# Hybrid encoder layer on one core: decay tables by column halves, q and k turned before they are split, side work on GpSimd

## The chip, the cores and the metric

The kernel runs on 1 core of one Trainium2 chip. The metric is the device time in microseconds (us) from launch to the end of the program; lower is better. Each kernel is timed in several runs, of which the median counts, and one further execution is profiled.

## The reference: what is computed

One encoder layer over 1024 tokens of width 1024 in float32. Only the middle part matters here:

```
u = x @ W_in  -> [q | k | v | z | x_ssd | B | C | dt_fwd | dt_bwd]
a = GQA(qk-RMSnorm, 2-D axial rotary, bidirectional)       # 8 query heads of 64, 2 key heads
s = bidirectional Mamba-2 SSD(conv, chunked scan per direction, summed, + D skip, SiLU(z) gated RMSNorm)
x = LN1(alpha*x + concat(a, s) @ W_out)
...
seg = a_cum[..., :, None] - a_cum[..., None, :]             # in each chunk of 128 tokens, each of 8 heads
Lmat = jnp.exp(jnp.where(tril, seg, -jnp.inf))              # the decays
y_diag = jnp.einsum('bcgls,bgrcls,bcsgrp->bclgrp', cb, Lmat, xd)
```

Ahead of it stands a SwiGLU block with a LayerNorm, behind it a second one, a gated embedding and the last LayerNorm. They take most of the time, and the change leaves them alone.

## The kernel before, in words

Matmuls of float32 accuracy are made of three single-pass products: each operand is split into a high part (a rounding copy, on ScalarE, written ACT in the profile) and a low part (the difference, `lo`, line 87, on VectorE, written DVE). `mm3` (line 122) issues high times low, low times high and high times high. TensorE (PE) follows the order in which the program is written: an `in_order` wrapper around the whole of `run` chains its instructions. The order on the other engines and on the DMA queue (SP) is set by a scheduler that plans with a simulated timeline; `behind` pins an instruction behind the last one traced on an engine. PSUM holds two pools: `big` with two buffers of two banks (`psb`) and `sm` with four buffers of one bank (`pss`).

**q and k** (`qkv_part`). Eight products of 128 tokens for q (512 columns, 24 matmuls each), then eight for k, v and dt (272 columns, 24 matmuls each). For each tile of tokens `step` runs the turn of an earlier tile, `front` (square, sum, power on GpSimd), the low part of an earlier tile and `back` (`rope`: Newton steps on the root, scaling by it at line 852, rotary). The result was split while tokens lay on the partitions: q into `qs` (high and low side by side), k into `kd`, where each head stands twice. Then `turn` transposed high and low together: eight transposes for a tile of q (line 901, into `big`), four for a tile of k (line 884, into `sm`), and one ScalarE copy brought them into Q (line 902) or K (line 885). A head of Q has its high part on partitions 0 to 63 and its low part on 64 to 127; K holds the high part on both halves for j = 0 and the low part for j = 1, so that two matmuls sum all four products.

**The convolved branch** (`xbc_part`) has eight products of 48 matmuls. The last turns of k ran between the halves of the first.

**Attention.** 64 steps of 128 queries of one head. A step has four score matmuls (line 1151), a maximum over 1024 keys on DVE (line 1158), the exponential on ACT (line 1160), the turn of an earlier step (eight transposes, line 1173, two ACT copies, two low parts on DVE) and a quarter of the product with V (lines 1188 and 1189). After four steps a head is done: ACT copies one half of the PSUM result to `a_tmp` (line 1195) and DVE adds the other (line 1196). After two heads GpSimd (POOL) spreads the reciprocal sums to `rx` (line 1201), and `normalise` turns them by a float32 matmul with the identity (line 1210); DVE multiplies (line 1211), POOL splits the result (lines 1213 and 1214). The list `aside` is worked off one entry in every second step, behind ACT and DVE: the SiLU of the last z tile (`one_more`, four reciprocals, `silu`), the SSD tables (`turned`, `masks`) and the splits of eight blocks of W_out.

**SSD, right to left** (`ssd_right`). For each of eight chunks and each direction a pair of banks got, for four heads at a time, a bf16 matmul of the identity with the mask (line 1342) and one of `LT` with `RT` (line 1343): 59 rows of the contraction carry the cumulative sums. ACT takes the exponential of 1024 columns (line 1345). Behind that come C times B (line 1349), the part from the state (lines 1262 and 1264), the next state (line 1273; its scaling on ACT at line 1256) and the product with x (line 1366). Products with half of W_out (`spilled`) lie between, two at the start and one at the end.

Of the kernel before, what the change touches and what calls it, by code (L numbers as in the profile page):

```python
# [9 lines left out]
F32 = mybir.dt.float32  # L10
F32R = mybir.dt.float32r
# [16 lines left out]
NQ = 8  # L28
# [8 lines left out]
class Layer:  # L37
# [778 lines left out]
    def qkv_part(self, c, xT):  # L816
# [30 lines left out]

        def rope(v, nh, m, ss, r, nm, t):

            self.newton(r, ss, nh)  # L850
            qn = wk.tile([P, nh, HD], F32, name="qn")
            nc.vector.tensor_tensor(out=qn, in0=v, in1=r.unsqueeze(2).broadcast_to([P, nh, HD]), op=ALU.mult)  # L852
# [8 lines left out]
            return qn  # L861

        NK = NKV * HD
        late = []

        def kv_front(t, ps):
# [5 lines left out]
            return st  # L872

        def kv_back(t, st):

            kn = rope(*st, "k", t).unsqueeze(2).broadcast_to([P, NKV, 2, HD])
            kd = wk.tile([P, NKV, 2, 2, HD], F32R, name="qs", bufs=4)
            nc.scalar.copy(out=kd[:, :, 0], in_=kn)

            def turn():  # L880
                pt = self.pss().rearrange("p (g j t) -> p g j t", g=NKV, j=2)
                for g in range(NKV):
                    for j in range(2):
                        nc.tensor.transpose(out=pt[:, g, j], in_=kd[:, g, j].rearrange("p a d -> p (a d)").bitcast(F32), identity=self.ident)  # L884
                nc.scalar.copy(out=K[:, :, :, t * P:(t + 1) * P], in_=pt)
            late.append(turn)
            return kd[:, :, 1], kn, kd[:, :, 0]

# [3 lines left out]
        def q_back(t, st):  # L892
            qs = wk.tile([P, NQ, 2, HD], F32R, name="qs", bufs=4)
            qn = rope(*st, "q", t)
            nc.scalar.copy(out=qs[:, :, 0], in_=qn)

            def turn():
                pt = self.psb().rearrange("p (h t) -> p h t", t=P)
                qv = qs.bitcast(F32)
                for hh in range(NQ):  # L900
                    nc.tensor.transpose(out=pt[:, hh], in_=qv[:, hh].rearrange("p a d -> p (a d)"), identity=self.ident)
                nc.scalar.copy(out=Q[:, :, t * P:(t + 1) * P], in_=pt)
            late.append(turn)
            return qs[:, :, 1], qn, qs[:, :, 0]

        backs, los = [], []

        def step(t, ps, front, back, keep=1):


            if len(late) > keep or not front:
                late.pop(0)()
            st = front(t, ps) if front else None
            if los:
                self.lo(*los.pop())
            if backs:
                los.append(backs.pop()())
            if front:
                backs.append(lambda: back(t, st))

# [11 lines left out]
        self.pend += [lambda: step(NT, None, None, None)] * 4  # L932
        self.x0 = self.xbc_gemm(0, xT, 1)
# [94 lines left out]
    def z_last(self, xT, aside):  # L1028

        nc, V = self.nc, self.nc.vector  # L1030
        ps = self.z_product(NT - 1, xT)
        r = self.ring.tile([P, 1024], F32, name="blk")
        z, e = r[:, :512], r[:, 512:]
        V.tensor_copy(z, ps)
        nc.scalar.activation(out=e, in_=ps, func=AF.Exp, scale=-1.0)

        def one_more():
            V.tensor_scalar(out=e, in0=e, scalar1=1.0, scalar2=None, op0=ALU.add)

        def invert(m):  # L1040
            V.reciprocal(e[:, m], e[:, m])

        def silu():
            V.tensor_tensor(out=z, in0=z, in1=e, op=ALU.mult)
            nc.sync.dma_start(out=self.zd[NT - 1], in_=z)
        aside += [one_more, *(lambda m=slice(i * P, (i + 1) * P): invert(m) for i in range(4)), silu]
# [78 lines left out]
    def attention(self, c, mixT, aside, begin):  # L1125
# [53 lines left out]
        def values(u, part):  # L1179
# [13 lines left out]
            raw, rsum = st[qh, hp]["raw"], st[qh, hp]["rsum"]  # L1193
            tmp = ev.tile([64, 512], F32, name="a_tmp")
# [9 lines left out]
        def normalise():  # L1204
            if "norm" not in st:
                return
            qh, hp, rx, raw = st.pop("norm")
            R = self.pss()
            for qt in range(4):
                nc.tensor.matmul(R[:, qt * P:(qt + 1) * P], lhsT=rx[:, qt].rearrange("p h d -> p (h d)"), rhs=self.ident, start=True, stop=True)  # L1210
            nc.vector.tensor_tensor(out=raw, in0=raw, in1=R, op=ALU.mult)
            hi, lo = (x[:, hp] for x in mixT[qh][0])
            nc.gpsimd.tensor_copy(hi, raw)
            nc.gpsimd.tensor_tensor(out=lo, in0=raw, in1=hi.bitcast(F32), op=ALU.subtract)
# [71 lines left out]
    def ssd_tables(self, pool):  # L1286


        nc, I, V = self.nc, self.I, self.nc.vector

        G = nc.gpsimd
        self.LT = LT = [pool.tile([P, NT, P], BF16, name=f"LT{d}") for d in range(2)]
        self.RT = [pool.tile([P, 8, P], BF16, name=f"RT{b}") for b in range(2)]
        self.mask = pool.tile([P, 2, P], BF16, name="mask")
        self.idb = pool.tile([P, P], BF16, name="idb")
        rraw, mraw = (self.ring.tile([P, 8, P], F32, name="blk") for n in range(2))
        nc.sync.dma_start(out=rraw[:59], in_=I["rows"])
        nc.sync.dma_start(out=mraw[:, :2], in_=I["mask"])
        for d in range(2):
            G.memset(LT[d], 0.0)  # L1300
            G.memset(LT[d][32 * d:32 * d + 3], 1.0)
            for i in range(3):
                nc.sync.dma_start(out=LT[d][32 * d + 3 + 8 * i:32 * d + 11 + 8 * i], in_=self.sc[1][d, i].rearrange("c h l -> h c l"))
        for b in range(2):
            G.memset(self.RT[b], 0.0)
        dsk = pool.tile([P, 16], F32, name="dsk")
        nc.sync.dma_start(out=dsk[:, :8], in_=I["d_skip"].broadcast_to([P, 8]))
        self.dsk = dsk[:, :8]

        def turned(ch):  # L1310
            V.tensor_copy(self.RT[ch % 2][:59], rraw[:59])
            self.rows(ch)

        def masks():
            V.tensor_copy(self.mask, mraw[:, :2])
            V.tensor_copy(self.idb, self.ident)
        return [lambda: turned(NT - 1), lambda: turned(NT - 2), masks]

    def ssd_right(self, c, loaded, fillers):
# [5 lines left out]
        self.accr = c.enter_context(tc.tile_pool(name="accr", bufs=2))  # L1325
        LT, RT, mask, idb, dsk = self.LT, self.RT, self.mask, self.idb, self.dsk
        for ch in (NT - 1, NT - 2):
            loaded[ch] = self.chunk(ch)

        def front(ch):  # L1330
# [7 lines left out]
            for d in range(2):  # L1338
                pD = self.psb()
                for n in range(2):  # L1340
                    o = pD[:, n * 512:(n + 1) * 512]
                    nc.tensor.matmul(o, lhsT=idb, rhs=mask[:, d].unsqueeze(1).broadcast_to([P, 4, P]), start=True, stop=False)
                    nc.tensor.matmul(o, lhsT=LT[d][:, ch], rhs=rt[:, n * 4:n * 4 + 4], start=False, stop=True)
                e = ep.tile([P, 8, P], F32, name=("Ef", "Eb")[d], bufs=2 + d)
                nc.scalar.activation(out=e.rearrange("p a b -> p (a b)"), in_=pD, func=AF.Exp)
                E.append(e)
# [179 lines left out]
    def run(self):  # L1526
# [37 lines left out]
        with ExitStack() as c:  # L1564
# [309 lines left out]
def host_arrays(inputs):  # L1874
# [54 lines left out]
    A["mask"] = c(np.stack([(1 - le) * np.float32(NEG), (1 - le.T) * np.float32(NEG)], 1))  # L1929
    rows = np.zeros((59, 8, P), np.float32)  # L1930
    for part in range(3):
# [27 lines left out]
```

## Time and profile before

| | |
|---|---|
| median of 3 runs | 1966.9 us (1966.21 to 1967.77) |
| span of the profiled execution, first to last instruction | 1962.3 us |
| q products, 715 to 766 us | PE busy 50.26 of 51 |
| k, v and dt products, 766 to 790 us | PE busy 23.47 of 24 |
| attention, one stretch of it, 900 to 940 us | PE 40.00 and DVE 39.94 of 40 |
| SSD right to left, 1070 to 1120 us | PE 50.00, ACT 42.86, DVE 40.01 of 50 |

The profiled execution has no time of its own beside its span; the median stands 4.6 us above the span, and this is what lies around it. A row of the timeline gives start, duration, engine, line, operation, output and inputs, the count where neighbours are merged, and in brackets the idle time ahead with what ended it. PE matmuls overlap in the records: a matmul shown with 0.39 us may be followed by the next after 0.23 us, so its price is the distance between starts. "SPq" is an issue on the DMA queue.

### The profile page before, as it was taken

The page shows a single profiled execution, that of the slowest core. Times are in us where ns is not written, and L with a number is a line of the kernel's source. Part 1 is how long each engine was busy: PE and PEld are TensorE (multiplying, and loading weights), DVE is VectorE, ACT ScalarE, POOL GpSimd, SP SyncE. Part 2 cuts the span into 40 slices and gives each one's busy share as a digit, 9 for nine tenths or more (in the row PEclk, how much of TensorE's full clock was granted, in tenths as well). Part 3 has the DMA queues.
Part 4 walks back from the last instruction along what each step waited for, and adds up shares of the span by engine and source line. Part 5 has one row for each costly group of instructions (what it writes and reads, how often), then busy time and mean ns, then how long its engine had stood idle before and what let it go on. Part 6 is the DMA issues. An engine that isn't in the chain of part 4 may idle for free.

```text
span 1962.3 us, 25749 instructions
## 1 busy us (share of the span) xinstructions
PE 1938.6 (99%) x9196; PEld 1614.3 (82%) x9196; DVE 1533.1 (78%) x2378; ACT 879.7 (45%) x1509; POOL 392.8 (20%) x292
## 2 busy tenths in 40 slices
PE   8999999999999999999999999999999999999998
PEld 7888888888888889888888888788888888888886
DVE  7977776867668658759998878997777777787698
ACT  7433333334444224538887775643333334443311
POOL 0144544430001132000101001003545440001011
PEclk9999999999999999999999999999999999999999
DMA  8434544559865112231003383253545439986122
GB/s 303 136 124 154 192 177 145 193 187 377 282 226 172 65 42 68 87 111 45 7 1 98 116 292 114 86 179 138 185 146 202 159 135 336 341 267 220 39 75 97
DMA packets 147180, 309.95 MB, mean 158 GB/s; under 512 B 17665, under 2 KB 30337, under 8 KB 147052
## 3 DMA queue, kind: packets, MB, share of 16 engines
q1 hardware_dynamic: 147052, 308.31, 44.9%
q8 instruction: 72, 1.18, 0.3%
q14 instruction: 56, 0.46, 0.1%
HBM read 216.83 MB, written 91.42 MB: 157 GB/s over the span
## 4 chain that ended last, share of the span: by engine, by line
PE 90%; DVE 6%; DMA 1%; POOL 1%; issue 1%; ACT 1%; SPq 0%; DVEq 0%; ACTq 0%; POOLq 0%
PE sm L122 56%; PE big L508 12%; PE sm L508 9%; PE big L122 3%; PE big L1151 2%; PE sm L1173 2%; DVE nm L1158 1%; PE sm L1188 1%; PE sm L1189 1%; POOL qr L845 1%; PE sm L1366 1%; PE sm L1262 1%; PE sm L1273 1%; DVE ptl L87 1%; DVE xl L87 1%
## 5 line engine op out<-in xcount | busy, mean ns | idle before, releaser
L122 PE MATMUL sm<-xh,blk 128*128 128x512 f32 x1424 | 439.9, 389 | 0.0
L122 PEld LDWEIGHTS sm<-xh,blk 128*128 128x128 f32 x1424 | 267.3, 188 | 55.4
L122 PE MATMUL sm<-xl,blk 128*128 128x512 f32 x736 | 283.9, 389 | 3.8 <-DVE xl L87 3.8
L122 PE MATMUL sm<-blk,xl 128*128 128x512 f32 (+2 forms) x784 | 238.4, 371 | 0.9 <-DVE qn L852 0.5
L122 PE MATMUL sm<-blk,xh 128*128 128x512 f32 (+2 forms) x584 | 202.7, 379 | 0.0
L108 ACT CAST blk<-raw 128x512 fp32r<-128x512 f32 (+1 forms) x168 | 101.1, 610 | 213.2 <-PE sm L122 128.6
L87 DVE TENSOR_TENSOR blk<-s,blk 128x512 fp32r<-128x512 f32 x176 | 152.1, 869 | 35.4 <-ACT blk L108 34.3
L87 DVE TENSOR_TENSOR blk<-raw,blk 128x512 fp32r<-128x512 f32 (+1 forms) x168 | 145.8, 871 | 37.9 <-ACT blk L108 37.5
L108 ACT CAST blk<-s 128x512 fp32r<-128x512 f32 x172 | 105.7, 622 | 138.9 <-PE sm L122 122.3
L122 PEld LDWEIGHTS sm<-xl,blk 128*128 128x128 f32 x736 | 138.2, 188 | 32.7 <-issue 4.2
L122 PEld LDWEIGHTS sm<-blk,xl 128*128 128x128 f32 x784 | 142.9, 188 | 25.3 <-PE sm L884 0.8
L178 POOL TENSOR_TENSOR ln_k<-ln_k,mhalf 128x1 f32<-128x1 f32 x32 | 36.9, 1158 | 583.2 <-DVE ln_k L177 578.2
L508 PE MATMUL big<-xh 128*128 128x512 f32 x576 | 138.8, 390 | 0.0
L267 POOL TENSOR_TENSOR s<-raw 128x512 f32<-128x512 f32 x34 | 55.1, 1621 | 387.4 <-DVE blk L87 294.3
L87 DVE TENSOR_TENSOR xh<-blk,xh 128x1024 fp32r<-128x1024 f32 x78 | 95.4, 1223 | 47.0 <-ACT xh L454 39.2
L454 ACT CAST xl<-blk 128x1024 fp32r<-128x1024 f32 x76 | 80.1, 1054 | 114.0 <-PE sm L508 43.2
L454 ACT CAST xh<-blk 128x1024 fp32r<-128x1024 f32 x78 | 82.2, 1054 | 106.7 <-PE big L508 47.4
L508 PEld LDWEIGHTS big<-xh 128*128 128x128 f32 x576 | 107.8, 188 | 22.2
L87 DVE TENSOR_TENSOR xl<-blk,xl 128x1024 fp32r<-128x1024 f32 x76 | 92.6, 1219 | 42.6 <-ACT xl L454 36.5
L122 PEld LDWEIGHTS sm<-blk,xh 128*128 128x128 f32 x584 | 109.8, 188 | 19.2
L508 PE MATMUL big<-xl 128*128 128x512 f32 x480 | 115.8, 390 | 0.0
L122 PE MATMUL sm<-xET3h,blk 128*128 128x512 f32 x352 | 108.4, 389 | 0.0
(339 smaller groups left out, 4025.3 us busy)
## 6 DMA issues: line engine op xcount, KB each, us to landing
raw<-in_wi_dram SPq DMA_DIRECT2D x81, 512.0 KB
blk<-hS SPq DMA_DIRECT2D x154, 256.0 KB
hS<-h SPq DMA_DIRECT2D x88, 256.0 KB
wr<-in_wo_dram SPq DMA_DIRECT2D x44, 512.0 KB
blk<-wT SPq DMA_DIRECT2D x88, 256.0 KB
hS<-sg SPq DMA_DIRECT2D x66, 256.0 KB
wT<-wr SPq DMA_DIRECT2D x66, 256.0 KB
blk<-in_wo_dram SPq DMA_DIRECT2D x66, 256.0 KB
```

The lines of the kernel that those rows point to most:

```text
L87: (eng or self.nc.vector).tensor_tensor(out=out, in0=full, in1=hi.bitcast(F32), op=ALU.subtract)
L108: self.nc.scalar.copy(out=b[:, 0, :n], in_=src)
L122: self.nc.tensor.matmul(ps, lhsT=a, rhs=b, start=(i == 0), stop=(i == n - 1))
L178: nc.gpsimd.tensor_tensor(out=r, in0=v, in1=self.mhalf[:, :1], op=ALU.pow)
L267: lambda: G.tensor_tensor(out=s1, in0=a21, in1=a22, op=ALU.add),
L454: A.copy(out=b[:, :, 0], in_=r)
L508: nc.tensor.matmul(ps[q], lhsT=b[:, 0, x, cut], rhs=b[:, 1, y], start=j == i == 0, stop=j == NP - 1 and i == 2)
L845: nc.gpsimd.tensor_tensor(out=r, in0=ss, in1=self.mhalf[:, :nh], op=ALU.pow)
L1151: nc.tensor.matmul(ps[:, n * 512:(n + 1) * 512], lhsT=Q[:, h, q0:q0 + P], rhs=K[:, h // 4, j, n * 512:(n + 1) * 512], start=j == 0, stop=j ...
L1158: nc.vector.tensor_reduce(out=nm, in_=ps, axis=AX.X, op=ALU.max, negate=True)
L1173: nc.tensor.transpose(out=pt[:, k], in_=pr[:, kk * P:(kk + 1) * P], identity=self.ident)
L1188: nc.tensor.matmul(po, lhsT=vw, rhs=pth[k // 4][:, k % 4], start=k == 0, stop=False)
```

## The change

- **q and k.** `rope` writes into a tile that is handed in and is split no more there. `turned` transposes four blocks of 128 columns of float32 into one `sm` buffer: a tile of q (four pairs of heads), or four tiles of k at once. ACT copies the high part from PSUM, and one step on, DVE takes the low part from PSUM; DMAs then put the pieces where Q and K want them: four for a tile of q (64 partitions, pieces of 512 bytes), eight for four tiles of k. Odd heads of Q now have the low part on top.
- **Attention.** ACT copies the other half of the result straight into `a_raw` in place of `a_tmp`. The sums are turned by a transpose in place of a matmul. `one_more`, `silu`, the copies for `RT`, the masks and the low parts of the eight blocks of W_out go to GpSimd.
- **Decays.** One matmul with all 128 rows serves all eight heads and half of the columns: rows 64 to 127 of `LT` hold the mask of that half and those of `RT` an identity, so the mask matmuls go. The exponential reads the banks as (half, head, column) and writes (head, half, column). `LT` has four tiles in place of two, with twelve DMAs in place of six.

```diff
+        def turned(blocks, place):
+            pt = self.pss()
+            for i, b in enumerate(blocks):
+                nc.tensor.transpose(out=pt[:, i * P:(i + 1) * P], in_=b, identity=self.ident)
+            hi, lo = (wk.tile([P, 512], F32R, name=n) for n in ("qhi", "qlo"))
+            nc.scalar.copy(out=hi, in_=pt)
+            def rest():
+                self.lo(lo, pt, hi)
+                for j, part in enumerate((hi, lo)):
+                    for e in range(2):
+                        for out in place(e, j):
+                            nc.sync.dma_start(out=out.bitcast(F32), in_=part[e * HD:(e + 1) * HD].bitcast(F32))
+            los.append(rest)
...
-            if len(late) > keep or not front:
+            if len(late) > keep:
                 late.pop(0)()
-            st = front(t, ps) if front else None
+            st = front(t, ps)
             if los:
-                self.lo(*los.pop())
+                los.pop()()
...
-            step(t, ps, kv_front, kv_back, 2)
+            step(t, ps, kv_front, kv_back, 1 if t < 2 else 0)
...
-            V.tensor_scalar(out=e, in0=e, scalar1=1.0, scalar2=None, op0=ALU.add)
+            nc.gpsimd.tensor_scalar(out=e, in0=e, scalar1=1.0, scalar2=None, op0=ALU.add)
...
-            nc.scalar.copy(out=tmp, in_=po[64:128])
-            nc.vector.tensor_tensor(out=raw[hh * 64:(hh + 1) * 64], in0=po[0:64], in1=tmp, op=ALU.add)
+            nc.scalar.copy(out=raw[mine], in_=po[other])
+            nc.vector.tensor_tensor(out=raw[mine], in0=po[mine], in1=raw[mine], op=ALU.add)
...
-                nc.tensor.matmul(R[:, qt * P:(qt + 1) * P], lhsT=rx[:, qt].rearrange("p h d -> p (h d)"), rhs=self.ident, start=True, stop=True)
+                nc.tensor.transpose(out=R[:, qt * P:(qt + 1) * P], in_=rx[:, qt].rearrange("p h d -> p (h d)"), identity=self.ident)
...
-                    nc.tensor.matmul(o, lhsT=idb, rhs=mask[:, d].unsqueeze(1).broadcast_to([P, 4, P]), start=True, stop=False)
-                    nc.tensor.matmul(o, lhsT=LT[d][:, ch], rhs=rt[:, n * 4:n * 4 + 4], start=False, stop=True)
+                    nc.tensor.matmul(pD[:, n * 512:(n + 1) * 512], lhsT=LT[d][n][:, ch], rhs=rt[:, :, n * 64:(n + 1) * 64], start=True, stop=True)
...
-                nc.scalar.activation(out=e.rearrange("p a b -> p (a b)"), in_=pD, func=AF.Exp)
+                nc.scalar.activation(out=e.rearrange("p h (n l) -> p n h l", n=2), in_=pD.rearrange("p (n h l) -> p n h l", n=2, h=8), func=AF.Exp)
...
-                aside.extend(lambda i=i, r=r: blocks0.append(self.split(r[:, i * 512:(i + 1) * 512])) for i in range(2) for r in early)
+                aside.extend(lambda i=i, r=r: blocks0.append(self.split(r[:, i * 512:(i + 1) * 512], eng=nc.gpsimd)) for i in range(2) for r in early)
```

More of the change, by code (lines that the diff above doesn't have):

```diff
@@ L872, in kv_front @@
             return st
+        kn = {}
         def kv_back(t, st):
[L876 to L887, printed above, removed]
+            h = t // 4
+            if t % 4 == 0:
+                kn[h] = wk.tile([P, 4, NKV, HD], F32, name="kn")
+            rope(kn[h][:, t % 4], *st, "k", t)
+            if t % 4 == 3:
+                cols = slice(h * 512, (h + 1) * 512)
+                late.append(lambda: turned([kn[h][:, i].rearrange("p g d -> p (g d)") for i in range(4)],
+                                           lambda g, j: [K[r * HD:(r + 1) * HD, g, j, cols] for r in range(2)]))
         def q_front(t, ps):
@@ L892, in q_back, with place @@
         def q_back(t, st):
[L893 to L906, printed above, removed]
+            qn = wk.tile([P, NQ, HD], F32, name="qn", bufs=4)
+            rope(qn, *st, "q", t)
+            Qv = Q.rearrange("p (i e) s -> p i e s", e=2)[:, :, :, t * P:(t + 1) * P]
+            def place(e, j):
+                r = e ^ j
+                return [Qv[r * HD:(r + 1) * HD, :, e]]
+            late.append(lambda: turned([qn[:, 2 * i:2 * i + 2].rearrange("p h d -> p (h d)") for i in range(4)], place))
         def step(t, ps, front, back, keep=1):
-            if len(late) > keep or not front:
+            if len(late) > keep:
                 late.pop(0)()
-            st = front(t, ps) if front else None
+            st = front(t, ps)
             if los:
-                self.lo(*los.pop())
+                los.pop()()
             if backs:
-                los.append(backs.pop()())
-            if front:
-                backs.append(lambda: back(t, st))
+                backs.pop()()
+            backs.append(lambda: back(t, st))
         tables("q", HD ** -0.5)
@@ L1286, in ssd_tables @@
     def ssd_tables(self, pool):
-        nc, I, V = self.nc, self.I, self.nc.vector
+        nc, I = self.nc, self.I
         G = nc.gpsimd
-        self.LT = LT = [pool.tile([P, NT, P], BF16, name=f"LT{d}") for d in range(2)]
+        self.LT = LT = [[pool.tile([P, NT, P], BF16, name=f"LT{d}{n}") for n in range(2)] for d in range(2)]
         self.RT = [pool.tile([P, 8, P], BF16, name=f"RT{b}") for b in range(2)]
-        self.mask = pool.tile([P, 2, P], BF16, name="mask")
-        self.idb = pool.tile([P, P], BF16, name="idb")
         rraw, mraw = (self.ring.tile([P, 8, P], F32, name="blk") for n in range(2))
-        nc.sync.dma_start(out=rraw[:59], in_=I["rows"])
-        nc.sync.dma_start(out=mraw[:, :2], in_=I["mask"])
+        nc.sync.dma_start(out=rraw, in_=I["rows"])
+        for n in range(2):
+            nc.sync.dma_start(out=mraw[64:, 2 * n:2 * n + 2], in_=I["mask"][64 * n:64 * n + 64])
         for d in range(2):
[L1300 to L1305, printed above, removed]
+            for n in range(2):
+                lt = LT[d][n]
+                G.memset(lt[:64], 0.0)
+                G.memset(lt[32 * d:32 * d + 3], 1.0)
+                for i in range(3):
+                    nc.sync.dma_start(out=lt[32 * d + 3 + 8 * i:32 * d + 11 + 8 * i], in_=self.sc[1][d, i].rearrange("c h l -> h c l"))
         dsk = pool.tile([P, 16], F32, name="dsk")
@@ L1310, in turned, with masks @@
         def turned(ch):
-            V.tensor_copy(self.RT[ch % 2][:59], rraw[:59])
+            G.tensor_copy(self.RT[ch % 2], rraw)
             self.rows(ch)
[L1314 to L1317, printed above, removed]
+        def masks(d):
+            for n in range(2):
+                G.tensor_copy(LT[d][n][64:], mraw[64:, 2 * n + 1 - d].unsqueeze(1).broadcast_to([64, NT, P]))
+        return [lambda: turned(NT - 1), lambda: turned(NT - 2), lambda: masks(0), lambda: masks(1)]
     def ssd_right(self, c, loaded, fillers):
@@ L1929, in host_arrays @@
     A["mask"] = c(np.stack([(1 - le) * np.float32(NEG), (1 - le.T) * np.float32(NEG)], 1))
-    rows = np.zeros((59, 8, P), np.float32)
+    rows = np.zeros((P, 8, P), np.float32)
+    for half in range(2):
+        rows[64 + np.arange(64), :, half * 64 + np.arange(64)] = 1.0
     for part in range(3):
```

15 lines of the change are left out of this document (6 added, 9 removed).

## The prediction, made before the result was known

> **What bounds the kernel now.** I read the page first, then the windows by stage, then the timeline of each stage that the diff touches.
>
> ```profile
> span 1962.3 us, 25749 instructions
> PE 1938.6 (99%) x9196; PEld 1614.3 (82%) x9196; DVE 1533.1 (78%) x2378; ACT 879.7 (45%) x1509; POOL 392.8 (20%) x292
> PE 90%; DVE 6%; DMA 1%; POOL 1%; issue 1%; ACT 1%; SPq 0%; DVEq 0%; ACTq 0%; POOLq 0%
> ```
> ```profile
> 900.00:940.00 40.00, 40.00 (x238) 33.73 (x236) 39.94 (x56) 32.95 (x62) 3.10 (x4) 1.00 0.02 8
> 1020.00:1070.00 50.00, 50.00 (x298) 42.73 (x297) 43.99 (x60) 39.05 (x71) 5.47 (x7) 1.00 0.18 53
> ```
>
> PE is busy 99% of the span and holds 90% of the chain that ended last, so a matmul taken out shortens the kernel unless another engine is nearly full in that stage. In a windows row the columns are length, then PE, PEld, DVE, ACT, POOL. DVE is full at 900 to 940 us and has slack at 1020 to 1070. PE's busy time overstates it, so I price every PE step by the distance between starts. The granted clock stays at 1.00 in these rows.
>
> **Turning q and k.**
>
> ```profile
> 732.97 1.03 PE L901 MATMUL big<-ident,qs 128*128 128x128 f32 x8
> 733.76 0.48 PE L122 MATMUL sm<-blk,xl 128*128 128x512 f32 x1
> ...
> 739.31 1.04 PE L901 MATMUL big<-ident,qs 128*128 128x128 f32 x8
> ...
> 769.62 0.60 PE L884 MATMUL sm<-ident,qs 128*128 128x128 f32 x4
> 769.97 0.37 PE L122 MATMUL sm<-blk,xl 128*128 128x272 f32 x1
> ```
>
> Eight transposes take 733.76 - 732.97 = 0.79 us, four 0.35. Each of the eight q tiles falls from eight to four: 8 x (0.79 - 0.35) = 3.5 us. For k, eight groups of four become two: 6 x 0.35 = 2.1 us, and the switch from transposes to another matmul costs PE something too, by estimate 0.05 a group. I take 2.4, bounds 2.1 and 2.6. The q step, 739.31 - 732.97 = 6.34 us, becomes 5.9.
>
> Two stalls of PE stand at the seam of q and k:
>
> ```profile
> 761.47 1.06 PE L901 MATMUL big<-ident,qs 128*128 128x128 f32 x8 [0.61 <-DVE qs L87]
> 766.53 0.36 PE L122 MATMUL sm<-blk,xl 128*128 128x272 f32 x1 [0.55 <-DVE qn L852]
> ```
>
> The first waits for a low part that the transposes no longer need; the second waits for a buffer of `sm`, and that pool now also holds what is turned of q. Steps get shorter, and the first turn of k comes one step behind its rope. I count the seam at nothing: at best both stalls go (1.2 us), at worst the first goes and the second comes four times as long (a loss of 1.1). The added DMAs, 8 x 4 and 2 x 8, go to SP behind low parts. Attention reads Q and K only behind the eight products of the convolved branch, so that transfer is covered; what the issues hold up is a rival below. ACT loses a copy of 1024 columns per q tile; GpSimd's power for the root is unchanged.
>
> **Attention.**
>
> ```profile
> 1030.74 1.08 PE L1151 MATMUL big<-K,Q 128*128 128x512 f32 x4
> ...
> 1033.47 1.08 PE L1151 MATMUL big<-K,Q 128*128 128x512 f32 x4
> ```
> ```profile
> 925.34 0.67 DVE L1211 TENSOR_TENSOR a_raw<-a_raw,sm 128x512 f32<-128x512 f32 x1
> ...
> 972.37 0.67 DVE L1211 TENSOR_TENSOR a_raw<-a_raw,sm 128x512 f32<-128x512 f32 x1
> ...
> 1004.34 1.21 DVE L1158 TENSOR_REDUCE nm<-big 128x1 f32<-128x1024 f32 x1
> ...
> 1006.66 1.21 DVE L1158 TENSOR_REDUCE nm<-big 128x1 f32<-128x1024 f32 x1
> ...
> 1040.10 0.68 DVE L1211 TENSOR_TENSOR a_raw<-a_raw,sm 128x512 f32<-128x512 f32 x1
> ...
> 1062.77 0.67 DVE L1211 TENSOR_TENSOR a_raw<-a_raw,sm 128x512 f32<-128x512 f32 x1
> ```
>
> A step costs PE 2.73 us and DVE 2.32. A pair of heads (eight steps) takes 1062.77 - 1040.10 = 22.67 us late in the stage, 0.83 more than 8 x 2.73: that is the normalising matmul, whose last instance shows as 0.89 below. As four transposes it costs 0.35 or 0.36: 8 x (0.83 - 0.36) = 3.8 us (4.3 by the 0.89).
>
> Early on, two pairs take 972.37 - 925.34 = 47.03 us in place of 45.34: work of the list `aside` fills DVE, and 1.7 us are lost. From DVE go the +1 and the product of the SiLU, two copies for RT, two entries of masks and eight low parts, 14 operations of some 0.68 (a row below), 9.5 us; four reciprocals stay, the first of them now behind GpSimd's +1, with DVE's maxima and so ACT's exponentials queued behind it; two steps, 5.5 us, lie between the two entries, and the +1 is shorter than the 1.31 below. DVE then needs 8 x 2.32 + 3 x 0.67 = 20.6 us per pair (two adds and a product beside the steps), plus the reciprocals in one pair, against 22.2 on PE. I take 1.7; bounds are 0 (the reciprocals alone hold PE) and 2.5 (the neighbouring pairs lost some too).
>
> GpSimd takes this on:
>
> ```profile
> L1210 PE MATMUL sm<-ident,rx x64: 270/275/275, 923.2 to 1070.7; 128*128 128x128 f32 x64
> ```
> ```profile
> 903.93 0.61 POOL L1201 COPY rx<-rinv 128x512 f32<-128x512 f32 x1 [122.94 <-DVE rinv L1199]
> ...
> 974.24 1.31 POOL L1214 TENSOR_TENSOR xl<-a_raw,xh 128x512 fp32r<-128x512 f32 x1
> ```
> ```profile
> 974.76 0.68 DVE L87 TENSOR_TENSOR xl<-sm,xl 128x512 fp32r<-128x512 f32 x1
> ```
>
> Its queue holds the spreading of the sums, which PE waits for, but that is done at 904.5 and first read at 923.2: 18 us of cover, against new entries of 0.6 to 1.3 us. Without that cover each late entry would cost PE up to 1.3. The new work is 0.6 + 1.3 for the SiLU, 8 x 1.31 for the low parts, and 6 copies of 1024 columns at twice 0.61: 19.7 us over 17 entries spaced 5.5 us.
>
> **Decays.**
>
> ```profile
> 1069.94 1.05 PE L1210 MATMUL sm<-ident,rx 128*128 128x128 f32 x8
> 1070.83 0.38 PE L1342 MATMUL big<-mask,idb 128*128 128x512 bf16 x1
> ...
> 1098.30 0.38 PE L1342 MATMUL big<-mask,idb 128*128 128x512 bf16 x1
> 1098.52 0.38 PE L1343 MATMUL big<-RT,LT 128*128 128x512 bf16 x1
> ...
> 1103.93 0.38 PE L1342 MATMUL big<-mask,idb 128*128 128x512 bf16 x1
> ...
> 1116.92 0.61 PE L1349 MATMUL sm<-bc 128*128 128x128 f32 x4
> ```
> ```profile
> 1088.10 1.02 ACT L1345 ACTIVATE Ef<-big 128x1024 f32<-128x1024 f32 x1 [2.42 <-PE big L1343]
> ...
> 1100.93 1.01 ACT L1345 ACTIVATE Ef<-big 128x1024 f32<-128x1024 f32 x1
> ...
> 1106.82 1.01 ACT L1345 ACTIVATE Ef<-big 128x1024 f32<-128x1024 f32 x1
> ...
> 1113.62 1.03 ACT L1345 ACTIVATE Eb<-big 128x1024 f32<-128x1024 f32 x1
> ```
>
> A mask matmul is worth 1098.52 - 1098.30 = 0.22 us (the last 0.01 is rounding; eight in a row take 1.72); four a chunk make 0.86, and 32 make 6.9. But the middle chunks come every 5.63 us on PE (1103.93 - 1098.30) and every 5.89 on ACT (1106.82 - 1100.93), which has no idle time there and was merely absorbing a backlog. Only the first three chunks, with ACT idle 2.42 us before 1088.10, pass on all: 3 x 0.86 = 2.6 us. From there ACT paces. For the last chunk, PE then waits until ACT has emptied the second pair of banks, at 1113.62 + 1.03 = 1114.65, and needs two matmuls, 0.43: 1115.08 in place of 1116.92, 1.8 us more. Together 4.4 us. Bounds: 2.6 (backlog not worked off) and 6.9 (ACT quicker than it looks). The product with W_out behind that chunk lets ACT catch up. The strided write of the exponential I price at nothing. Six more small loads of `LT` on SP and its tables' memsets on POOL come before attention, and the tables are read first at 1070.83: covered.
>
> The Trainium skill (TensorE: Matmul & The Clock Gate, Back-to-back issue gap) gives about 131 ns for a sustained 512-column matmul; by it the masks would be worth an estimated 32 x 0.131 = 4.2 us before any cap. The starts 0.215 us apart disagree, and the row decides.
>
> **The sum** is 3.5 + 2.4 + 0 + 3.8 + 1.7 + 4.4 = 15.8 us off the span of 1962.3: 1946.5. The median of the runs, 1966.9, stands 4.6 above that span; with the same outside it: 1951.1.
>
> **Rivals.** (a) *`sm` runs short.* A q product that ended at 732.97 was read at
>
> ```profile
> 740.97 0.69 DVE L852 TENSOR_TENSOR qn<-sm,qr 128x512 f32<-128x512 f32 x1
> ```
>
> so it holds a bank for 5.5 + 8.7 = 14.2 us. At 5.9 a step that is three banks, and the turned tile takes the fourth: it just fits. If buffers go round strictly, every second one belongs to turned tiles, a product waits for the one two before, and the step is 14.2 / 2 = 7.1 us: 1.2 more over five q steps, and some 0.7 over three of k: 8 us, giving 1959.1.
>
> (b) *GpSimd locks DVE out.* The Trainium skill (SBUF — State Buffer, SBUF: two separate sides) says that a DVE operation with two SBUF inputs and a GpSimd operation that reads SBUF exclude each other. The first feed-forward block agrees:
>
> ```profile
> 308.91 1.62 POOL L268 TENSOR_TENSOR s<-s,raw 128x512 f32<-128x512 f32 x1
> ```
> ```profile
> 309.30 1.78 DVE L87 TENSOR_TENSOR blk<-s,blk 128x512 fp32r<-128x512 f32 x1
> ```
>
> If all of DVE's work in attention were held so, 19.7 us of GpSimd against 9.5 relieved would add 10.2 there in place of saving 1.7: 1951.1 + 11.9 = 1963.0, at the edge of what can be told. Against it: at 974.76 a low part with one input in PSUM took 0.68 inside GpSimd's 1.31.
>
> (c) *SP holds the weight loads: slower.*
>
> ```profile
> 744.83 0.33 SPq L94 DMA_DIRECT2D raw<-in_wkv_dram  x1
> 746.50 38.89 SPq L94 DMA_DIRECT2D raw<-in_wx_dram  x7
> ```
> ```profile
> 747.55 0.74 ACT L108 CAST blk<-raw 128x272 fp32r<-128x272 f32 x2 [1.88 <-DMA raw<-in_wkv_dram]
> ```
>
> The wkv load was split at 747.55, for a product that runs from 749.81: 2.3 us of cover. If stores that wait for a low part stand ahead of the loads and hold each by one q step, 5.9 us, PE waits 3.6 per load. From the fifth of these eight loads on the gain is gone; six cost 21.6: 1951.1 + 21.6 = 1972.7. Against it: the second row shows seven loads in 39 us, so SP has room for the stores, and the planner queues a store when it expects it ready.
>
> (d) *ACT does not bind:* all 6.9 us, 1948.6. That lies in the forecast's own range: every upper bound together (3.5 + 2.6 + 1.2 + 4.3 + 2.5 + 6.9 = 21.0) gives 1945.9, every lower one (3.5 + 2.1 - 1.1 + 3.8 + 0 + 2.6 = 10.9) gives 1956.0.
>
> **Chances.** Forecast with (d) 0.74; (a) 0.12; (b) 0.06; (c) 0.05; something unseen 0.03. The range, 1945.5 to 1960, holds the forecast's own and (a). About 0.2%, 4 us, is what a measurement of this kernel can tell from no change. Faster by more: forecast, (a) and part of the unseen, 0.87. Same: (b), 0.07. Slower: (c), 0.06.
>
> **What would show it.** After: line 901 and 884 gone and 40 transposes in one helper; q steps of 5.9 us; L1210 in 32 records; pairs of heads all near 22.2 us; no mask matmuls; ACT exponentials 5.9 us apart from the fourth chunk on, with PE waiting for ACT there. I am wrong if PE waits for `sm` in the q steps, if DVE's low parts in attention rise above 0.7 us, if exponentials take longer than 1.03, or if ACT waits for weight loads behind SP.

## The result and the profile after

The changed kernel takes 1973.09 us (median of 5 runs, 1972.34 to 1976.69), the kernel before 1967.77 (5 runs beside them): a ratio of 1.0034, interval 1.0022 to 1.0046. The change makes the kernel 0.34% slower; forecast were 1951.1 us, in a range that ended at 1960. The profiled execution of the changed kernel took 1972.97 us with a span of 1971.2: 1.8 us lie around the span. The executions of the kernel before have the same 1.8, so its profiled execution (1962.3) was some 2.5 us quicker than its median: of the 4.6 us that were taken to lie around its span, only 1.8 do.

The page after: engine totals, busy tenths of PE, granted clock, chain.

```profile
span 1971.2 us, 25587 instructions
PE 1930.1 (98%) x9076; PEld 1607.7 (82%) x9076; DVE 1527.3 (77%) x2358; ACT 865.0 (44%) x1486; POOL 415.2 (21%) x310
PE   8999999999999999799999899999999999999998
PEclk9999999999999999899999999999999999999999
PE 94%; DVE 3%; DMA 1%; issue 1%; ACT 1%; SPq 0%; DVEq 0%; ACTq 0%
```

PE is busy 8.5 us less than before, as meant, and the span is 8.9 us longer. The row of PE has a new 7 in its 17th slice (788 to 838 us), with an 8 in the clock's, and an 8 in the 23rd (1084 to 1133). So the loss has places; it isn't spread over the kernel.

The stages follow from the first start of each group of matmuls. Groups of the changed kernel:

```profile
L868 PE MATMUL sm<-ident,qn x32: 270/273/299, 721.7 to 759.9; 128*128 128x128 f32 x32
L1155 PE MATMUL big<-K,Q x256: 387/393/504, 890.6 to 1066.5; 128*128 128x512 f32 x128
L1344 PE MATMUL big<-RT,LT x32: 378/379/391, 1077.3 to 1123.0; 128*128 128x512 bf16 x32
L1673 PE MATMUL big<-ident,acc x64: 270/273/273, 1204.1 to 1241.4; 128*128 128x128 f32 x64
```

| us | before | after | with the fix `k_pool` (below) |
|---|---|---|---|
| to the first turn of q | 720.3 | 721.7 | 720.9 |
| q, k, v and the convolved branch, to the first score product | 159.2 | 168.9 | 156.3 |
| attention, to the first product of the decays | 191.3 | 186.7 | 186.6 |
| right-to-left pass and what lies between, to the next transposes of `acc` | 125.4 | 126.8 | 125.2 |
| the rest of the span | 766.1 | 767.1 | 768.1 |

The first and the last row are untouched code and differ by 1 to 2 us from one profiled execution to the next. The second row holds the loss: 9.7 us longer in place of 5.9 shorter.

In that stage, VectorE, SP and PE of the changed kernel, one fence each:

```profile
788.97 0.68 DVE L87 TENSOR_TENSOR qlo<-sm,qhi 128x512 fp32r<-128x512 f32 x1
795.98 0.23 DVE L1063 TENSOR_SCALAR pm<-dt 128x128 f32<-128x128 f32 x1 [6.32 <-DMA K<-qlo]
...
800.11 1.28 DVE L973 SCALAR_TENSOR_TENSOR conv<-big,cw,conv 128x1022 f32<-128x1022 f32 x1
```
```profile
788.85 2.39 SPq L877 DMA_DIRECT2D K<-qhi  x4
791.28 2.52 SPq L877 DMA_DIRECT2D K<-qlo  x4
793.85 0.59 SPq L94 DMA_DIRECT2D raw<-in_wx_dram  x1
795.77 0.33 SPq L961 DMA_DIRECT2D cw<-in_cw_dram  x1
```
```profile
808.62 0.77 PE L122 MATMUL big<-xh,blk 128*128 128x512 f32 x1 [9.58 <-DVE conv L973]
```

The reader is to see a DVE instruction that has nothing to do with K, the first of `ssd_prep` (it scales `dt`), wait 6.32 us for a transfer out of `qlo`. It waits for the *space*: `qhi` and `qlo` come from the pool `qwork`, which closes with the projections, and the tiles opened next lie where it was. Half of K is turned at the end of the first product of the convolved branch, and its eight stores, 0.6 us an issue, end late. The convolution, the only reader of the two `big` buffers, comes behind, and PE stands still for 9.58 us. Then the clock is low:

```profile
799.00:808.60 9.60, 0.04 (x1) 0.01 (x1) 9.60 (x15) 2.75 (x5) 0.00 (x0) 0.61 0.17 56
808.60:812.00 3.40, 3.38 (x8) 2.73 (x9) 3.33 (x7) 2.94 (x3) 0.00 (x0) 0.50 0.00 0
812.00:816.00 4.00, 4.00 (x13) 3.11 (x13) 1.84 (x9) 2.00 (x3) 0.00 (x0) 0.65 0.00 0
816.00:820.00 4.00, 4.00 (x19) 3.30 (x18) 0.00 (x0) 0.01 (x1) 0.00 (x0) 1.00 0.00 0
```

The granted clock (the third number from the end) is 0.50: from 808.62 to 814.30 PE issues 13 matmuls, which at the pace ahead of the stall (three in 0.68 us) take 3.0 us in place of 5.7. That is 2.7 more, some 12.3 us at this place.

The second loss is at the seam of q and k. PE's waits there, 0.17 and the four below, add up to 3.6 us, where the kernel before had 1.2:

```profile
753.44 0.63 PE L868 MATMUL sm<-ident,qn 128*128 128x128 f32 x4 [0.39 <-DVE rs_t L130]
754.82 0.39 PE L122 MATMUL sm<-blk,xl 128*128 128x272 f32 x1 [0.76 <-DVE qn L851]
759.57 0.63 PE L868 MATMUL sm<-ident,qn 128*128 128x128 f32 x4 [1.48 <-DVE qn L859]
761.02 0.39 PE L122 MATMUL sm<-blk,xl 128*128 128x272 f32 x1 [0.82 <-DVE kn L851]
```

The third is in the right-to-left pass: the mask matmuls are gone, and PE waits for the state instead.

```profile
1110.87 1.20 PE L1266 MATMUL sm<-state,bc 128*128 128x256 f32 x4 [2.74 <-DVE state L1283]
1118.81 1.13 PE L1266 MATMUL sm<-state,bc 128*128 128x256 f32 x4 [1.27 <-DVE state L1283]
1125.12 1.13 PE L1266 MATMUL sm<-state,bc 128*128 128x256 f32 x4 [1.28 <-DVE state L1283]
```

### The profile page after: what moved, and what is told of

Its sections match the earlier page's. It is cut to its first block, busy times and chain, and to the rows that moved or that the text cites. A ratio compares the mean times of both kernels' runs of the same rounds, so it can differ in the third digit from the quotient of the medians.

```text
span 1971.2 us, 25587 instructions
## 1 busy us (share of the span) xinstructions
PE 1930.1 (98%) x9076; PEld 1607.7 (82%) x9076; DVE 1527.3 (77%) x2358; ACT 865.0 (44%) x1486; POOL 415.2 (21%) x310
## 4 chain that ended last, share of the span: by engine, by line
PE 94%; DVE 3%; DMA 1%; issue 1%; ACT 1%; SPq 0%; DVEq 0%; ACTq 0%
PE sm L122 58%; PE big L508 12%; PE sm L508 9%; PE big L122 3%; PE big L1155 3%; PE sm L1177 2%; PE sm L1192 1%; PE sm L1193 1%; PE sm L1266 1%; PE sm L1367 1%; PE sm L1277 1%; DVE nm L1162 0%; DVE conv L973 0%; PE big L224 0%; PE big L1673 0%
## 5 line engine op out<-in xcount | busy, mean ns | idle before, releaser
L508 PEld LDWEIGHTS big<-xh 128*128 128x128 f32 x576 | 107.9, 188 | 22.2
L122 PE MATMUL sm<-xET2h,blk 128*128 128x512 f32 x352 | 108.4, 390 | 0.0
```

The lines of the kernel that those rows point to most:

```text
L122: self.nc.tensor.matmul(ps, lhsT=a, rhs=b, start=(i == 0), stop=(i == n - 1))
L508: nc.tensor.matmul(ps[q], lhsT=b[:, 0, x, cut], rhs=b[:, 1, y], start=j == i == 0, stop=j == NP - 1 and i == 2)
```

## The experiments

Medians are of 5 to 11 runs; ratios are against the kernel before, timed beside them (1966.3 to 1966.5 us).

### Which part, and is it the space?

`k_pool`, the changed kernel with

```diff
+        kt = ExitStack()
+        self.turns = kt.enter_context(tc.tile_pool(name="kturn", bufs=1))
         with ExitStack() as c2:
             self.qkv_part(c2, xT)
...
+        kt.close()                     # behind the convolved branch
...
-            hi, lo = (wk.tile([P, 512], F32R, name=n) for n in ("qhi", "qlo"))
+            hi, lo = (pool.tile([P, 512], F32R, name=n) for n in ("qhi", "qlo"))   # pool: turns for K's second half
```

> The changed kernel, with one edit: the two tiles from which the second half of K is stored (`qhi` and `qlo` of the last turn) come from a pool of their own, which stays open until the convolved branch is done. Their space is then not handed on to the first step of `ssd_prep`. Nothing else differs, the stores stand at the same place of SP's queue. Theory (the space of these tiles is reused, so VectorE's first operation of `ssd_prep` waits until the stores have landed, the convolution queues behind it, both `big` buffers stay full and TensorE stands still): VectorE's wait of 6.32 us before `pm` and TensorE's of 9.58 us go, and with them some 4 us at a reduced granted clock: 1973.1 - 13.6 = 1959.5, between 1958 and 1963. Rival (SP's eight issues of 0.6 us hold back weight loads, and that is what the stage waits for): the issues are still there, so no change, 1973. Rival (`sm` runs short): no change either.

Measured: 1960.06 us, 13.0 less than the changed kernel (12.8 by the two ratios to the kernel before) and 0.9969 of the kernel before (0.9958 to 0.9981). VectorE and SP at the same place:

```profile
787.23 0.23 DVE L1066 TENSOR_SCALAR pm<-dt 128x128 f32<-128x128 f32 x1 [0.65 <-PE sm L871]
...
788.26 0.68 DVE L87 TENSOR_TENSOR qlo<-sm,qhi 128x512 fp32r<-128x512 f32 x1
...
791.18 1.25 DVE L976 SCALAR_TENSOR_TENSOR conv<-big,cw,conv 128x1022 f32<-128x1022 f32 x1
```
```profile
787.22 0.33 SPq L964 DMA_DIRECT2D cw<-in_cw_dram  x1
...
788.07 2.38 SPq L880 DMA_DIRECT2D K<-qhi  x4
790.55 2.48 SPq L880 DMA_DIRECT2D K<-qlo  x4
```

The eight stores are still there and take as long. What they no longer hold is the first operation of `ssd_prep`, and also the load of the convolution's coefficients `cw`, which now stands ahead of them; in the changed kernel it stood behind them, 1.3 us after the issue before it had ended.

The three parts of the change, each alone on the kernel before:

> The kernel before, with the part on q and k alone (attention and decays as before). Theory: PE's q and k steps are 5.9 us cheaper, 3.6 us of that go to new stalls at the seam, and the wait for K's stores costs 13.6: about 11 slower than before, 1979, with attention starting some 10 to 11 us later than in the kernel before. Had the loss come from the attention or the decays: 1962.

> The kernel before, with the part on attention alone (transposes for the spreading of the sums, side work on GpSimd, the copy for the odd head). The traces differ by 4.6 us in that stage: 1967.8 - 4.6 = 1963. The prediction's own price was 5.5: 1962. If GpSimd held VectorE back, no gain: 1968 or more.

> The kernel before, with the part on the decays alone; it also has the copy for the odd head of attention (one ScalarE copy per head pair without a tile of its own), since the larger tables need that space. Theory (ScalarE and the state's chain set the pace behind the third chunk, whatever PE saves): between 1 us faster and 2 slower than before, 1967 to 1970. Rival (the mask matmuls were on the path, and what the changed kernel lost there was only the late start or the other parts): 4.4 faster, 1963.

| part alone | us | ratio and interval |
|---|---|---|
| q and k | 1980.81 | 1.0073 (1.0060 to 1.0087) |
| attention | 1963.38 | 0.9985 (0.9976 to 0.9994) |
| decays | 1962.42 | 0.9983 (0.9975 to 0.9992) |

Differences to 1966.4 of +14.4, -3.0 and -4.0 add up to +7.4, against +5.3 for the whole change; the copy for the odd head is in both smaller parts. The whole loss is that of q and k: its trace has the same hole, 9.60 us, and one further wait of PE, 2.30 us for a low part of the weights of k and v. The decays were worth 4.0 alone, near the 4.4 that the prediction had priced and against the theory I had taken from the trace after. But the stage itself, first decay product to the `acc` transposes, lasts 124.7 us there in place of 125.4; the rest came in the two stages ahead of it (157.4 in place of 159.2 and 189.8 in place of 191.3), where this kernel's copies for `RT` and masks are off VectorE too and PE's stalls at the seam, which this part doesn't touch, were absent. So the 4.0 does not confirm the price: the stage that was priced gave 0.7.

### Who else holds the same space

Three kernels leave the stores in the space of `qwork` and move what waits for them. `prep_late` starts `ssd_prep` behind the second product in the program's order, `prep_behind` pins it behind the first convolution on VectorE's queue, and `cw_behind` loads `cw` early into another pool as well.

```diff
-            if j in (0, 2):                       # prep_late: (1, 3)
-                next(prep, None)
+            if j in (0, 2):
+                with self.behind(mybir.EngineType.DVE):
+                    next(prep, None)
```

> The changed kernel, with one edit and no other memory: the two steps of `ssd_prep` are started behind the second and fourth product of the convolved branch in place of the first and third. The tiles of K's stores come from the same space as before. Theory (VectorE's queue is held by the wait of `ssd_prep` for these stores): the first convolution now stands ahead of the waiting operation, and the stores have landed when it comes up, so the loss goes as it did with the pool of its own: about 1960, between 1958 and 1964. Rival (the other tiles of the stage, those of the convolution above all, lie on that space too and wait likewise): 1970 or more.

> The changed kernel, with one edit and no other memory: the first step of `ssd_prep` is put behind the first convolution on VectorE's queue by an explicit order (moving its place in the program, as in prep_late, left the queue's order as it was). It still waits for K's stores. Theory (what costs is that the convolution is queued behind the waiting operation): the stores land while the convolution runs, nothing is held up, and the loss goes: 1958 to 1964. Rival (the convolution's own tiles wait for the stores too): 1970 or more.

> As prep_behind, and one more edit: the coefficients `cw` of the convolution lie in the pool of Q and K and are loaded before the projections, so neither VectorE's queue nor the first convolution touches the space of K's stores. Theory (that space is all that held the stage): the first convolution starts as soon as its product is there, some 790 us into the run, and the 13 us are back: 1958 to 1963. Rival (the load of the next weight block, which SP issues behind the eight stores and whose split stands ahead of the convolution on ScalarE): the convolution starts at some 796.6 in place of 797.9, and 1 to 3 us are back: 1969 to 1971.

Measured: 1974.3 us (1.0036), 1972.41 (1.0032) and 1968.84 (1.0009, interval 1.0000 to 1.0018). In `prep_late` the scheduler put `pm` where it had been, so that run told only that the program's order isn't the queue's. In `prep_behind` VectorE no longer waits for the stores, but PE still stands still for 8.74 us, and almost nothing is won. In `cw_behind` PE's wait is down to 5.51 us. ACT of these two:

```profile
796.00 0.62 ACT L108 CAST blk<-raw 128x512 fp32r<-128x512 f32 x1 [7.58 <-PE big L122]
797.92 1.20 ACT L968 ACTIVATE conv<-big,cw 128x1024 f32<-128x1024 f32 x1 [1.30 <-DMA pa<-in_a_log_dram]
```
```profile
794.36 1.21 ACT L968 ACTIVATE conv<-big,cw 128x1024 f32<-128x1024 f32 x1 [6.98 <-DMA K<-qlo]
795.47 0.61 ACT L108 CAST blk<-raw 128x512 fp32r<-128x512 f32 x1
```

With VectorE's queue free, ACT is late with the split of the weight block, whose load SP issued at 793.45, behind the stores (the profile names PE, which had long been done), and then waits for the last of the small loads (`cw` was issued at 795.38, `pa` right behind it). With the coefficients out of the way too, the convolution's own tile waits for K's stores: it lies on the same space. So there are three holders one behind the other, `pm`, `cw` and `conv`, and each hides the next. My expectation for `cw_behind` (all 13 us back) failed because of the third; the rival, the weight load, is not what was late there, since its split comes behind the convolution. Space of its own for the stores removes all three at once.

`two_queues` asks what makes the stores so long; low parts go by GpSimd's queue: `(nc.sync, nc.gpsimd)[j].dma_start(...)`.

> The changed kernel, with one edit: the low parts of q and k are stored through GpSimd's queue in place of SP's, the high parts stay on SP. Theory (VectorE waits until the last of eight stores has landed, and SP takes 0.6 us for each of the eight issues): four issues run beside the other four, the last store lands some 2.4 us earlier, so VectorE's wait falls from 6.3 to 3.9, PE's from 9.6 to 7.2: 1970 to 1971. Rival (the transfer itself takes the time, not the issue): no change, 1973. Second rival (GpSimd's queue is slower, and holds the power for the roots behind stores): 1975 or more.

Measured: 1976.46 us (1.0046, 1.0033 to 1.0058); in the profiled execution, the quickest of the five with 1971.93 us, VectorE's wait is 8.35 us and PE's 11.61. GpSimd and VectorE:

```profile
790.17 2.10 POOL L877 DMA_DIRECT2D K<-qlo  x4 [10.65 <-DVE qlo L87]
```
```profile
798.23 0.23 DVE L1063 TENSOR_SCALAR pm<-dt 128x128 f32<-128x128 f32 x1 [8.35 <-DMA K<-qlo]
```

From the end of the last issue to the released VectorE operation are 798.23 - 792.27 = 6.0 us; on SP it was 795.98 - 793.80 = 2.2. The issues ended 1.5 us earlier, the data landed later. My theory missed; the second rival was right about the slower queue. That the roots are held up behind the stores doesn't show: between 715 and 800 us VectorE waits 2.8 us for them, and 6.7 in the changed kernel.

### The seam of q and k

On top of `k_pool`, `q_big` turns q into a buffer of `big`, and `seam` also turns the last two tiles one k step later.

```diff
-            pt = self.pss()
+            pt = self.psb()[:, :512] if big else self.pss()
...
-            step(t, ps, kv_front, kv_back, 1 if t < 2 else 0)
+            step(t, ps, kv_front, kv_back, (2, 1, 1, 0)[min(t, 3)])     # seam only
```

> The kernel with a pool of its own for K's stores, and one more edit: the turned q goes to a buffer of `big` (idle in this stage) and not of `sm`. Theory for the seam of q and k (3.3 us of waits of PE between 749 and 765 us): 1.8 us of them are for a buffer of `sm`, the rival (a) of the prediction on a smaller scale, and go; the 1.5 us in which a turn waits for the rotation of its q stay: 1958.3. Rival (VectorE is late there, whatever the buffer): no change, 1960.

> As q_big, and the last two turns of q come one k step later (up to two outstanding turns are kept in the first k step, one in the next two, none from there). Theory: both kinds of wait at the seam go, 3.3 us: 1956.8. Rival: VectorE is full at the seam and hands the delay on to the k steps: as q_big or slower, 1958 to 1960.

Measured: 1961.16 us (0.9975) and 1961.09 (0.9973): neither gains on 1960.06. The waits of PE move, and their sum grows from 3.3 us to 4.1 in `q_big` and 4.7 in `seam`. In `q_big` one turn alone waits

```profile
759.59 1.09 PE L871 MATMUL big<-ident,qn 128*128 128x128 f32 x4 [2.45 <-DVE qn L862]
```

and in `seam` a k product waits 2.5 us for its buffer and k's turn 1.6 for `kn`. In `k_pool` VectorE is busy 11.77 of the 13 us from 747 to 760, with the splits of the next weights, the tables for k and the low parts of q; it is late there, whichever buffer PE writes. So the short supply of `sm`, rival (a), is not what costs at the seam.

Another 1.00 us of these 13 is the main fault once more, on a smaller scale: a low part of q waits until an earlier store out of `qlo`, which has two buffers, has landed, and the rotation that the turn needs is queued behind it. VectorE and PE of `k_pool`:

```profile
755.15 0.69 DVE L87 TENSOR_TENSOR qlo<-sm,qhi 128x512 fp32r<-128x512 f32 x1 [1.00 <-DMA Q<-qlo]
```
```profile
758.65 0.63 PE L871 MATMUL sm<-ident,qn 128*128 128x128 f32 x4 [1.25 <-DVE qn L862]
```

In all eleven profiles that have the changed q and k with the seam and the store queue unaltered, this turn waits 0.22 to 0.26 us longer than VectorE waits for that store, from 1.00 and 1.25 us here to 2.22 and 2.47 in `xs_y_pool`. So the largest wait at the seam follows the stores of q. More buffers for `qhi` and `qlo` were not tried; what they would win is open.

### The right-to-left pass

Five kernels, all on `k_pool`: `y5` has five `y` buffers, `xs_pool` scales x for the state on GpSimd in place of ACT, `xs_y_pool` makes `y` there too, `state_first` writes the next state ahead of the chunk's other work, `xs_y_first` has both.

```diff
-        self.scale_heads(xs, xb, self.sdt[:, ch, d * 8:d * 8 + 8])                   # xs_pool
+        nc.gpsimd.tensor_tensor(out=self.heads(xs), in0=self.heads(xb[:, :512]), in1=self.per_head(self.sdt[:, ch, 8:16]), op=ALU.mult)
...
+                new = self.next_state(two, st, 1, c1, xb) if c1 > 0 else None        # state_first
                 B[c1] = (c1, xb, bc) + mid(c1, xb, bc, E, cb)
...
-                if c1 > 0:
-                    st = self.next_state(two, st, 1, c1, xb)
+                st = new
```

> The kernel with a pool of its own for K's stores, and one more edit: five buffers of `y` in place of three in the right-hand pass over the chunks. Theory: VectorE's wait of 1.40 us for a `y` that is still being stored goes, and the sum of the state, queued behind it, comes earlier; ScalarE (5.9 us a chunk) still sets the mean pace: up to 1.4 us faster, 1958.7 to 1960. Rival (VectorE's order and that wait, not ScalarE, are what the chain of states hangs on): 3 us or more faster, 1957 or less.

> The kernel with a pool of its own for K's stores, and one more edit: in the right-hand pass over the chunks, the scaling of x for the next state (eight ScalarE operations a chunk, 1.92 us of its 5.9) is one operation on GpSimd. Theory (ScalarE sets the pace in this stage, and for that reason the mask matmuls brought 0.2 us of the 4.4 forecast, or 6.9 at most): the chunks come closer together, down to what PE or the chain of states needs, and the stage is 3 to 6 us shorter: 1955 to 1957. Rival (the chain of states sets the pace: product, VectorE's sum, ScalarE's scaling): the stage stays within 1 us, 1960. Second rival: GpSimd's operation is so slow, or holds VectorE so much, that the stage gets longer: 1962 or more.

> As xs_pool, and one more edit: the product of x with the skip weights (`y`, one VectorE operation a chunk, 0.60 us) goes to GpSimd as well, with four buffers of `y`. Per chunk that leaves PE 4.77, VectorE 4.7, ScalarE 4.0, GpSimd some 2.4 to 3 us. Theory (behind ScalarE, VectorE's 5.3 us a chunk and its order is the next bound): the chunks come up to 0.6 us closer on the last five, 2 to 3 us in all: 1955.5 to 1956.5. Rival (a GpSimd operation and a VectorE operation with two operands in SBUF exclude each other, as `y` with 1.53 in place of 0.68 us beside GpSimd's `xs` showed): no gain or a loss against xs_pool, 1958.4 to 1961.

> The kernel with a pool of its own for K's stores, and one more edit: in the right-hand pass over the chunks the next state is written down ahead of the work on the chunk's decays, so the order of the queues puts the state's scaling and sum earlier. Theory (ScalarE, 5.9 us a chunk, sets the pace; the order only moves the waits about): within 1 us, 1959.5 to 1960.5. Rival (the state's sum comes late because VectorE does the chunk's other work first): 2 to 4 us faster, 1956 to 1958.

> As xs_y_pool with the edit of state_first. If ScalarE and the order both held the chunks, the two gains add up: 1954 to 1955.5. If the lock between GpSimd and VectorE or VectorE's own load is the bound now: as xs_y_pool, 1956.3.

| kernel | us | ratio and interval | stage in its profile (before: 125.4) |
|---|---|---|---|
| `k_pool` | 1960.06 | 0.9969 (0.9958 to 0.9981) | 125.2 |
| `y5` | 1959.43 | 0.9965 (0.9951 to 0.9979) | 127.0 |
| `xs_pool` | 1958.40 | 0.9959 (0.9947 to 0.9972) | 123.4 |
| `xs_y_pool` | 1956.31 | 0.9951 (0.9939 to 0.9964) | 123.1 |
| `state_first` | 1957.24 | 0.9954 (0.9940 to 0.9967) | 122.5 |
| `xs_y_first` | 1955.57 | 0.9948 (0.9935 to 0.9960) | 120.5 |

Eight profiles have this pass as it is in `k_pool`; their stage lasts 124.7 to 128.6 us. Order alone, with no work taken off ACT, brings 2.7 us of the stage against `k_pool`, the relief of ACT 1.8; both end below all eight, but which of them brings more is not decided. The queue of VectorE in `k_pool` shows why, and behind it PE's wait:

```profile
1093.80 0.69 DVE L1360 TENSOR_TENSOR y<-xb,dsk 128x512 f32<-128x512 f32 x1 [1.40 <-DMA yd<-y]
1094.41 0.68 DVE L1272 TENSOR_TENSOR y<-y,toff 128x512 f32<-128x512 f32 x1
1095.01 1.22 DVE L1361 TENSOR_TENSOR Eb<-Eb,Ef 128x1024 f32<-128x1024 f32 x1
1096.15 0.68 DVE L1371 TENSOR_TENSOR y<-y,sm 128x512 f32<-128x512 f32 x1
1096.74 0.68 DVE L1286 TENSOR_TENSOR state<-state,sm 128x512 f32<-128x512 f32 x1
```
```profile
1097.57 1.10 PE L1269 MATMUL sm<-state,bc 128*128 128x256 f32 x4 [2.84 <-DVE state L1286]
```

The state's sum, on which the next chunk's product hangs, stands behind four other operations, the first of which waits 1.40 us until an earlier `y` has been stored. More buffers did not help: in `y5` VectorE waits 0.94 us for `xb` instead, the sum still comes late, and PE waits 3.42 us for it. With the state written first (`state_first`), PE runs chunks three to seven 4.77 us apart (in `k_pool` three to six, and the seventh comes 7.8 behind the sixth), while ACT starts the exponentials of chunks three to five 5.9 apart; PE waits for the state only from the seventh chunk on (2.8 us in two waits):

```profile
1080.94 1.04 PE L1347 MATMUL big<-RT,LT 128*128 128x512 bf16 x4
1085.72 1.03 PE L1347 MATMUL big<-RT,LT 128*128 128x512 bf16 x4
...
1095.25 1.03 PE L1347 MATMUL big<-RT,LT 128*128 128x512 bf16 x4
1100.02 1.12 PE L1347 MATMUL big<-RT,LT 128*128 128x512 bf16 x4
```
```profile
1081.58 1.02 ACT L1349 ACTIVATE Ef<-big 128x1024 f32<-128x1024 f32 x1 [0.58 <-PE big L1347]
...
1087.49 1.01 ACT L1349 ACTIVATE Ef<-big 128x1024 f32<-128x1024 f32 x1
```

My theory for this stage, that ACT's pace was the whole of it, was half of the story. Together, the order and the relief bring 4.7 us of the stage (125.2 to 120.5), and `xs_y_first` has the lowest median, 1955.57 us: faster than the kernel before by 0.5% and than the changed one by some 17 us. Within the table the medians decide little: the intervals of neighbours overlap, and even those of `xs_y_first` and `k_pool` just touch (0.9960 and 0.9958).

## Why the prediction was wrong, point by point

- **The step that failed:** "Attention reads Q and K only behind the eight products of the convolved branch, so that transfer is covered". The readers of the *destination* were rightly looked up; the transfer is covered for them. The next user of the *source*'s space was not. A copy that ACT had written straight into K became a store out of a tile whose pool closes at once, and three things that are opened on that space wait for its landing. Measured: 13.0 us (`k_pool`), against a price of zero. Without it the kernel takes 1960.06, just above the end of the range. Of the 9.0 us that are left to the forecast, the next three points make up 8.0 by the profile of `k_pool` (3.0, 0.8 and 4.2).
- **Turning q and k, 5.9 us.** The q step is 5.9 us as said (721.66, 727.56, 733.48). In `k_pool` the stage is 2.9 shorter. PE's waits at the seam rose from 1.2 to 3.3 us, a loss of 2.1 where zero was taken and 1.1 was the worst bound (1.0 by its own two rows). The other 0.9 are not accounted for, and the same code takes 156.2 to 159.3 us in six profiles. A buffer of `big` for the turned q won nothing; VectorE is nearly full there, and the largest wait follows a store that still holds `qlo`, as in the first point.
- **Attention, 5.5 us.** Right: 4.6 in the trace. Pairs of heads are 22.25 us apart throughout, 22.2 were forecast; PE never waits for GpSimd, though its +1 took 1.50 us where 0.6 was counted. Alone, the part measured 3.0 (1.2 to 4.7 by its interval); there VectorE keeps the copies for `RT` and the masks.
- **Decays, 4.4 us (bounds 2.6 and 6.9).** The stage kept 0.2 in `k_pool` and lost 1.4 in the changed kernel, where the granted clock was 0.65 in the 3.2 us behind a wait of 2.74. That ACT does 5.9 us a chunk was right; that PE would wait for nothing but ACT was not: it waits for the state, whose sum stands late in VectorE's queue, and that queue was left out. With the order mended (`state_first`) the stage gains 2.9, inside the bounds.
- **Rivals.** (c), slower for the weight loads behind SP's stores, gave 1972.7, almost the measured time, but by another way: ACT's waits for `in_wx` were 2.6 us at the longest, and in `k_pool`, with the same issues in the queue, the loss is gone. On a small scale `qk_alone` looks like it: SP issued the load of wkv at 745.66, right behind two stores of q that had waited for their low part, and PE waited 2.30 us for the low part of wkv. No run tests that. (a) costs nothing measurable: `q_big` gained nothing. (b): one pair shows GpSimd held while VectorE reads two operands from SBUF, POOL and DVE of the changed kernel:

```profile
1079.91 2.38 POOL L1218 TENSOR_TENSOR xl<-a_raw,xh 128x512 fp32r<-128x512 f32 x1
```
```profile
1079.90 1.22 DVE L1358 TENSOR_TENSOR Eb<-Eb,Ef 128x1024 f32<-128x1024 f32 x1 [0.75 <-ACT Eb L1346]
```

GpSimd's low part takes 2.38 us beside VectorE's 1.22, where 1.31 was its time alone. The rule that the prediction quoted from the Trainium skill (SBUF — State Buffer, SBUF: two separate sides) agrees with this pair. In attention it cost nothing that shows: GpSimd's low parts took 1.29 to 1.31 us there, and most of VectorE's operations have one operand in PSUM. (d) did not occur.

## What to carry to other kernels

When an engine's copy becomes a DMA, ask two questions of it: who reads what it writes, and who gets the space that it reads from. A store that is harmless for its destination still holds its source until it has landed, and whatever comes next into that space, a later pool's tile or the next round of its own buffer, waits with it on its engine or queue. And when such a wait is moved and nothing is won, look for the next holder of the same space before giving up the theory.

## What the runs showed of the hardware

- **An idle PE may come back at half clock.** After idle times of 9.58 us (changed kernel), 3.42 (`y5`) and 5.51 (`cw_behind`) the granted clock was 0.50 or 0.51 in the next 3.4 us, and after 2.45 (`q_big`), 2.74 (changed kernel) and 2.12 (`state_first`) it was 0.52, 0.65 and 0.81 over the next 3.2 to 3.4 us. But after 2.84 us in `k_pool` it stayed at 1.00. Length alone does not settle it. Behind the longest stall it cost 2.7 us on top, so a stall of PE should be priced with more than its length. The Trainium skill (TensorE: Matmul & The Clock Gate, What's actually happening) states a window of about 3.4 us that runs free of the program, full speed after one busy window and half speed after at least one idle one. The half speed agrees, and so does the time at it (some 5.7 us after the longest stall is longer than one window, within two); that idle times of 2.12 to 2.74 us, shorter than the window, were enough, does not.
- **A store through GpSimd's queue landed later than one through SP's**: 6.0 against 2.2 us from the end of the last issue to the operation it released, for the same four pieces. The Trainium skill (DMA: Bandwidth & Descriptors, Specifications) gives the GpSimd path a first byte after about 1 us and the other after about 0.6; the direction agrees, the measured gap of 3.8 us is larger.
